# Vector operands in PSUM, another order of projections and state tiles out of the weight buffers, in a hybrid decoder step on eight cores

## The chip, the cores and the metric

One Trainium2 chip, all eight cores, the same program on each with its own sequences. The metric is the device time in microseconds (us) of the slowest core.

## The reference, cut to what matters

```python
hn = rmsnorm(x, norm1_g)
proj = hn @ w_in                        # [u | B | C | h], 2048 wide
ya = pool_mixer(u)                      # causal means of 2, 4, 8, 16 rows
yb = B * conv3(C * h)                   # gated short convolution
x  = x + concat(ya, yb) @ w_out
a  = relu(rmsnorm(x, norm2_g) @ w1)     # 1024 -> 4096
x  = x + (a * a) @ w2
y  = rmsnorm(x, final_g)
# also out: the last 15 rows of u and the last 2 of C*h per sequence (the state)
```

A core has 2128 columns (tokens), cut into five groups of 512, 480, 496, 480 and 160. All activations stay in SBUF.

## The kernel before: the parts that matter

The kernel records operations with the memory they read and write. A small scheduler derives the semaphore waits and orders each engine's queue by a cost model. TensorE keeps the program's order. A transfer's wait stands in the queue of the engine that issues it, in order with that engine's other work (in the profile before, POOL stood idle for 4.0 us until the store of npp had landed, and only then issued its next weight load).

```python
# SBUF: the weight buffers of the MLP reuse the memory of the mixer phase
R0 = cur[0]
WIN = tile((16, 8, 128), BF16); WOUT = tile((8, 1024), BF16)
HN = ...; UB = ...; UC = tile((4, 16), F32); SP = ...; ZB = ...; ZC = tile((4, 8), F32)   # state rows UC, ZC
W1B = [tile((8, 8, 128), BF16, at=R0 + i * 16384) for i in range(2)]          # over WIN
W2B = [tile((8, 1024), BF16, at=R0 + 32768 + i * 16384) for i in range(2)]    # [0] over WOUT, [1] over HN, UB, UC
A2 = ...                                                                     # over SP, ZB, ZC
# ... cut
def bank():                      # eight rotating PSUM banks
    b = nbank[0] % 8
# ... cut
def rstd(s, hl, rs, n, rq=None): # sum of squares -> broadcast by ones-matmul -> Ln, Exp, into SBUF (rs)
def conv(c, z, h, s, n, cv):     # c: block, cv: accumulator in SBUF
    act(cv, z(h - 2 * s, h - 2 * s + n), scale=cw(0, c))                       # ACT
    stt(cv, z(h - s, h - s + n), cw(1, c), cv, ALU.mult, ALU.add)              # DVE
    stt(cv, z(h, h + n), cw(2, c), cv, ALU.mult, ALU.add)                      # DVE
# ... cut
# IN(g): 16 projections; evacuations are held until the norm is known (hook), then released
IN(1, {4: lambda: rstd1(1), 9: lambda: norm1(2), 12: ..., 13: ...}, 4, 4)
# ... cut: after IN(4): store UC -> npp, ZC -> ncp (the state of the prompt)
def w1_step(...):
    act(r, bk(0, n), AF.Relu)                                                  # ACT, PSUM -> SBUF
    tt(a2[fc, 0:n], r, r, ALU.mult)                                            # DVE
def finish(g):                   # final norm
    for k in range(8):
        if k % 2:
            act(x, x, scale=fg(k))
            tt(x, x, RSF[0:n], ALU.mult, eng="gpsimd")                         # POOL
        else:
            stt(x, x, fg(k), RSF[0:n], ALU.mult, ALU.mult)                     # DVE
```

TensorE's order is IN(0), IN(1), OUT(0), IN(2), OUT(1), IN(3), OUT(2), IN(4), OUT(3), OUT(4), then 20 steps of W1 and 20 of W2 (four blocks of weights by five groups, W2 one step behind W1), with the final norms in the last steps.

## Time and profile before

| | before |
|---|---|
| time, median of the first 6 runs | 699.41 us (697.98 to 781.55, the last a slow run by its time) |
| spans of the cores in the profiled run | 691.7 to 698.8 us |
| PE / DVE / ACT / POOL busy on the slowest core | 659.8 / 403.6 / 234.2 / 185.6 us |

PE is TensorE's matmuls, DVE VectorE, ACT ScalarE, POOL GpSimd. PSUM is the memory that the matmuls write; the kernel uses it as eight banks of 512 columns, and evacuating a bank means reading it out so that the next projection may have it. The granted clock is the share of TensorE's full clock that the trace records. PE is nearly full, so the useful question is where it is not. The prediction cuts the span by stretches. To compare kernels I use a second cut, made from the traces: all 3,589 weight loads of PE are in each trace, in program order, so the n-th belongs to the same matmul of the same stage in both kernels, projections aside. A stage begins at the start of its first weight load; each start is the median over the eight cores, and a stage is the difference of two such starts.

### The profile page before, as it was taken

To read this page: it belongs to the slowest core of one execution; us is meant where nothing else is said; L and a number is where in the kernel's file an instruction comes from. 1 tells how busy PE (TensorE), PEld (TensorE's weight loads), DVE (VectorE), ACT (ScalarE), POOL (GpSimd) and SP (SyncE) were. 2 spreads that over 40 slices of the span, in tenths; PEclk is the share of its full clock that TensorE was granted. 3 is DMA by queue.
4 is the path that set the end of the run, shared out by engine and by line. 5 is a ranking of instruction groups with operands and counts; after the bars stand their busy time and mean duration, and the time that the engine had idled before them with its cause. 6 is when DMAs were issued, how large, how long until landed. Compare 5 with 4: busy or idle time off the path is not lost.

```text
span 698.8 us, 11070 instructions; the slowest of 8 cores (691.7 to 698.8 us)
## 1 busy us (share of the span) xinstructions
PE 659.8 (94%) x3586; PEld 333.6 (48%) x3589; DVE 403.6 (58%) x630; ACT 234.2 (34%) x503; POOL 185.6 (27%) x177
## 2 busy tenths in 40 slices
PE   6998999899899699999999999999999999999964
PEld 2343444344664244445644446464444655444444
DVE  4598789998892643444433444344434443475676
ACT  4585546254444202101221121121211122544553
POOL 0347859172754000001000001000000000454784
PEclk9999999999999889999999999999999999999996
DMA  8997030100199900006060002332000000030215
GB/s 248 322 290 140 1 113 12 60 0 2 30 141 153 163 1 1 0 2 121 1 121 1 0 1 44 78 60 62 1 1 1 1 1 2 0 117 1 113 63 206
DMA packets 14679, 46.76 MB, mean 67 GB/s; under 512 B 3360, under 2 KB 5920, under 8 KB 13344
## 3 DMA queue, kind: packets, MB, share of 16 engines
q0 software_dynamic: 4032, 18.88, 16.2%
q1 hardware_dynamic: 10592, 27.19, 11.9%
q8 instruction: 30, 0.49, 0.3%
q14 instruction: 25, 0.20, 0.1%
HBM read 55.69 MB, written 9.24 MB: 93 GB/s over the span
## 4 chain that ended last, share of the span: by engine, by line
PE 75%; DMA 12%; DVE 5%; issue 4%; ACT 2%; POOL 1%; DVEq 0%; ACTq 0%; SPq 0%; POOLq 0%
PE psall L385 75%; DMA big<-w 4%; DMA npp<-big 3%; DVE big L400 3%; DMA big<-w_in 2%; DVE big L409 2%; ACT big L395 2%; DMA big<-x 1%; POOL big L400 1%; DMA big<-w0c 1%; ACT big L433 0%; ACT L433 0%; DVE big L427 0%; DVEq L229 0%; DVEq L248 0%
## 5 line engine op out<-in xcount | busy, mean ns | idle before, releaser
L385 PE MATMUL psall<-big 128*128 128x480 bf16 (+3 forms) x3586 | 659.8, 346 | 33.2 <-DVE big L400 10.6
L385 PEld LDWEIGHTS psall<-big 128*128 128x128 bf16 x3589 | 333.6, 99 | 359.0 <-issue 58.0
L400 POOL TENSOR_TENSOR big<-big 128x496 f32<-128x496 f32 (+8 forms) x141 | 165.6, 1189 | 243.7 <-ACT big L395 219.0
L400 DVE TENSOR_TENSOR big<-psall,big 128x480 f32<-128x480 f32 (+7 forms) x256 | 146.6, 589 | 120.0 <-PE psall L385 110.9
L400 DVE TENSOR_TENSOR big<-big 128x496 bf16<-128x496 f32 (+5 forms) x193 | 126.6, 662 | 152.3 <-ACT big L395 142.3
L395 ACT ACTIVATE big<-psall 128x480 f32<-128x480 f32 (+5 forms) x215 | 107.9, 512 | 316.6 <-PE psall L385 296.8
L395 ACT ACTIVATE big<-big 128x480 f32<-128x480 f32 (+9 forms) x203 | 110.1, 566 | 115.6 <-DVE big L400 75.8
L409 DVE SCALAR_TENSOR_TENSOR big<-big 128x496 bf16<-128x496 f32 (+9 forms) x151 | 121.9, 847 | 9.6 <-POOL big L400 4.3
L439 POOL DMA_DIRECT2D big<-w x24 | 13.0, 545 | 239.5 <-PE psall L385 235.2
L433 ACT COPY big<-big 128x16 f32<-128x16 f32 (+1 forms) x72 | 12.4, 191 | 14.8 <-DVE big L409 6.1
L427 DVE TENSOR_TENSOR_SCAN big<-big 128x480 f32<-128x480 f32 (+3 forms) x10 | 13.7, 1375 | 3.3 <-ACT big L395 3.3
L433 ACT CAST big<-big 128x1024 bf16<-128x1024 f32 x12 | 12.4, 1042 | 6.4 <-DMA big<-w_in 6.4
L434 POOL CAST big<-big 128x1024 bf16<-128x1024 f32 x4 | 4.9, 1214 | 26.9 <-DMA big<-w_in 26.9
L418 DVE TENSOR_SCALAR big<-big 128x512 bf16<-128x512 f32 (+2 forms) x16 | 6.7, 439 | 6.4 <-DMA big<-w0c 4.4
L433 ACT ACT_TABLE_LOAD x1 | 1.3, 1283 | 6.3 <-DMA big<-w0c 6.3
L439 POOL DMA_DIRECT2D big<-w_out x4 | 2.3, 582 | 0.0
L484 DVE MEMSET big<- 128x512 bf16 x1 | 0.5, 485 | 1.2 <-PEq L264 1.2
L264 POOL MEMSET const-float32-0.0<- 128x1 f32 x1 | 0.1, 98 | 0.5 <-issue 0.5
L483 DVE MEMSET big<- 128x128 bf16 x1 | 0.2, 165 | 0.0
L777 DVE MEMSET big<- 128x128 f32 x1 | 0.2, 165 | 0.0
L264 POOL MEMSET const-bfloat16-1.0<- 128x1 bf16 x1 | 0.1, 101 | 0.0
L264 POOL MEMSET const-uint8-127<- 128x1 uint8 x1 | 0.1, 101 | 0.0
(2 smaller groups left out, 0.2 us busy)
## 6 DMA issues: line engine op xcount, KB each, us to landing
big<-w POOLq DMA_DIRECT2D x16, 512.0 KB, 11.2
big<-w POOLq DMA_DIRECT2D x8, 1024.0 KB, 17.7
big<-w_in SPq DMA_DIRECT2D x15, 512.0 KB, 9.7
y<-big SPq DMA_DIRECT2D x8, 496.0 KB, 2.8
y<-big SPq DMA_DIRECT2D x8, 480.0 KB, 2.6
big<-x SPq DMA_DIRECT2D x4, 512.0 KB, 9.1
big<-w_out POOLq DMA_DIRECT2D x4, 512.0 KB, 15.2
big<-x SPq DMA_DIRECT2D x1, 1984.0 KB, 11.2
```

The source lines that it names most:

```text
L264: nc = bass.Bass("TRN2", target_bir_lowering=False)
L385: return P.add("tensor", lambda e: e.matmul(out=out.ap, lhsT=w.ap, rhs=x.ap, start=start, stop=stop), reads=[w, x], writes=[out], cost=pas ...
L395: return P.add("scalar", lambda e: e.activation(out=out.ap, in_=in_.ap, func=func, scale=sc, **kw), reads=reads, writes=[out], cost=0.155 ...
L400: return P.add(eng, lambda e: e.tensor_tensor(out=out.ap, in0=a.ap, in1=b.ap, op=op), reads=[a, b], writes=[out], cost=cost)
L409: return P.add("vector", lambda e: e.scalar_tensor_tensor(out=out.ap, in0=a.ap, scalar=sv, in1=b.ap, op0=op0, op1=op1), reads=reads, write ...
L418: return P.add(eng, lambda e: e.tensor_scalar(out=out.ap, in0=a.ap, scalar1=sv, scalar2=None, op0=ALU.mult), reads=reads, writes=[out], co ...
L427: return P.add("vector", lambda e: e.tensor_tensor_scan(out=out.ap, data0=a.ap, data1=b.ap, initial=iv, op0=ALU.add, op1=ALU.subtract), re ...
L433: return P.add(eng, lambda e: e.copy(out=out.ap, in_=a.ap), reads=[a], writes=[out], cost=0.17 + n / 1180)
L434: return P.add(eng, lambda e: e.tensor_copy(out=out.ap, in_=a.ap), reads=[a], writes=[out], cost=0.15 + n / 960)
L439: op = P.add(q, lambda e: e.dma_start(out=out.ap, in_=src), writes=[out], cost=0.6 if q == "gpsimd" else 0.6, dma=True, nbytes=nbytes, aft ...
L483: P.add("vector", lambda e: e.memset(ONES[:].ap, 1.0 / D), writes=[ONES[:]], cost=0.2)
L484: P.add("vector", lambda e: e.memset(A2[0][0].ap, 0.0), writes=[A2[0][0]], cost=0.3)
```

## The change

Its intent: let DVE read and write PSUM where it read two operands from SBUF, so that its instructions no longer stretch beside POOL's (in the profile before, over all cores, 94 products of 480 columns with both operands in SBUF took 1.04 us on average with POOL busy for over 60% of their time, and 146 took 0.70 with it idle); load the second half of the network's weights without waiting for small stores; release PSUM early in group 1; shorten the tail. The core of the diff:

```diff
-E_ORDER = (3, 8, 12, 2, 9, 13, 4, 1, 10, 14, 5, 0, 11, 15, 6, 7)
+E_ORDER = (8, 12, 9, 13, 3, 2, 4, 10, 14, 5, 1, 11, 15, 6, 0, 7)
     ONES = tile((128,), BF16)
+    UC = tile((4, 16), F32)
+    ZC = tile((4, 8), F32)
     R0 = cur[0]
...
+    def bank():
+        nbank[0] += 1
+        return fixed(nbank[0] % 5)
+    NB = [fixed(5), fixed(6)]
+    CVB = fixed(7)
...
-            out = SP[c - 2, NMAX - nt:NMAX]
-            scan(out, ub(16, L), ub(16 - w, L - w), ini)
+            scan(NB[1](0, nt), raw or ub(16, L), ub(16 - w, L - w), 0.0 if g == 0 else SC[c - 2])
...
-    def conv(c, z, h, s, n, cv):
-        act(cv, z(h - 2 * s, h - 2 * s + n), scale=cw(0, c))
+    def conv(c, z, h, s, n, cv, acc):                  # acc: in bank CVB
+        act(acc, z(h - 2 * s, h - 2 * s + n), scale=cw(0, c))
...
+        raw = (2, 3) if g == 1 else ()                 # evacuated before the norm is known
...
-            stt(H2[g][k, 0:n], X[g][k, nm:nm + n], g2(k), R2N[0:n], ALU.mult, ALU.mult)
+            stt(H2[g][k, 0:n], X[g][k, nm:nm + n], g2(k), NB[0](0, n), ALU.mult, ALU.mult)
...
-            tt(a2[fc, 0:n], r, r, ALU.mult)
+            tt(a2[fc, 0:n], bk(0, n), r, ALU.mult)
...
+            if b < 2:                                  # W2 of blocks 0, 1 in order on the queue
+                if pw2[0] is not None:
+                    op.deps.setdefault(pw2[0], False)
+                pw2[0] = op
...
-            if k % 2:
-                act(x, x, scale=fg(k))
-                tt(x, x, RSF[0:n], ALU.mult, eng="gpsimd")
-            else:
-                stt(x, x, fg(k), RSF[0:n], ALU.mult, ALU.mult)
+            stt(x, x, fg(k), NB[g % 2](0, n), ALU.mult, ALU.mult)
```

Cut: two engines that read one PSUM bank are now ordered, the scheduler's model has DVE without a PSUM operand and POOL take turns (its simplification) and a slower first stretch of DMA (in the profile before 266 GB/s from 2 to 13 us, 319 from 13 to 40), and the hooks of IN(0) and IN(1) move by one.

More of the change, by code (lines that the diff above doesn't have):

```diff
@@ L99 @@
 class Op:
-    __slots__ = ("eng", "fn", "deps", "cost", "dma", "idx", "n", "succ", "alap", "sig", "count", "nbytes", "end", "raw")
+    __slots__ = ("eng", "fn", "deps", "cost", "dma", "idx", "n", "succ", "alap", "sig", "count", "nbytes", "end", "port")
 class Prog:
@@ L118, in add @@
         op.sig = False
+        op.port = not dma and (eng == "gpsimd" or eng == "vector" and not any(
+            isinstance(c, tuple) for v in reads for c in v.cells))
         deps = {}
@@ L124, in add @@
                     deps[o] = True
+                if isinstance(c, tuple):
+                    for o in self.r.get(c, ()):
+                        if o.eng != eng:
+                            deps[o] = True
         for v in writes:
@@ L170, in schedule @@
         dma_free = 0.0
+        port = [0.0]
         for o in ops:
@@ L194, in schedule @@
             _, _, o = heapq.heappop(avail[e])
+            if o.port:
+                t = max(t, port[0])
+                port[0] = t + o.cost
             free[e] = t + o.cost
             if o.dma:
-                dma_free = max(dma_free, t + o.cost + 1.6) + o.nbytes / 330e3
+                dma_free = max(dma_free, t + o.cost + 1.6) + o.nbytes / (260e3 if dma_free < 13 else 335e3)
                 o.end = dma_free + 0.7
@@ L311, in build_nc @@
     UB = tile((2, 16 + NMAX), F32)
-    UC = tile((4, 16), F32)
-    SP = tile((2, NMAX), F32)
+    SC = tile((2, 1), F32)
     ZB = tile((2, 8 + NMAX), F32)
-    ZC = tile((4, 8), F32)
     CGB = tile((2, NMAX), F32)
@@ L325, in build_nc @@
     R1N = tile((2, NMAX), F32)
-    R2N = tile((NMAX,), F32)
     assert cur[0] <= SBUF_BYTES, cur[0]
@@ L357, in build_nc @@
     HLF = tile((2, NMAX), BF16, at=o + 8 * NMAX)
-    RSFB = tile((2, NMAX), F32, at=o + 12 * NMAX)
-    o += 20 * NMAX
+    o += 12 * NMAX
     SQL = tile((2, NOUT[NG - 1]), F32, at=o)
@@ L371, in build_nc, with fixed @@
     nbank = [0]
-    def bank():
-        b = nbank[0] % 8
-        nbank[0] += 1
+    def fixed(b):
         def view(lo, hi):
@@ L398, in tt @@
     def tt(out, a, b, op=ALU.add, eng="vector"):
-        cost = 0.15 + out.n / 950 if eng == "vector" else 0.15 + out.n * 2.25e-3
+        cost = 0.15 + out.n / 950 if eng == "vector" else 0.15 + out.n * 1.8e-3
         return P.add(eng, lambda e: e.tensor_tensor(out=out.ap, in0=a.ap, in1=b.ap, op=op),
@@ L409, in stt @@
         return P.add("vector", lambda e: e.scalar_tensor_tensor(out=out.ap, in0=a.ap, scalar=sv, in1=b.ap, op0=op0, op1=op1),
-                     reads=reads, writes=[out], cost=0.2 + out.n / 950)
+                     reads=reads, writes=[out], cost=0.15 + out.n / 950)
     def ts(out, a, s, eng="vector"):
@@ L503, in sumsq, with rstd, pool_sum @@
             tt(s[0:n], s[0:n], b, eng=eng)
-    def rstd(s, hl, rs, n, rq=None):
+    def rstd(s, hl, n, rs=None, rq=None, b=NB[0]):
         act(hl[0, 0:n], s[0:n])
         tt(hl[1, 0:n], s[0:n], hl[0, 0:n], ALU.subtract)
-        b = bank()
         mm(b(0, n), ONES[:], hl[0, 0:n], True, False)
         mm(b(0, n), ONES[:], hl[1, 0:n], False, True)
-        act(rs, b(0, n), AF.Ln, bias=EPS)
+        act(b(0, n), b(0, n), AF.Ln, bias=EPS)
         if rq is not None:
-            act(rq, rs, AF.Exp, scale=-1.0)
-        act(rs, rs, AF.Exp, scale=-0.5)
-    def pool_sum(g, c, ub, h, n, nt, mix):
+            act(rq, b(0, n), AF.Exp, scale=-1.0)
+        act(rs or b(0, n), b(0, n), AF.Exp, scale=-0.5)
+    def pool_sum(g, c, ub, h, n, nt, mix, raw):
         w = POOL_WIN[c]
@@ L527, in pool_sum @@
         else:
-            out = SP[c - 2, NMAX - nt:NMAX]
-            ini = 0.0 if g == 0 else SP[c - 2, NMAX - 1:NMAX]
-            scan(out, ub(16, L), ub(16 - w, L - w), ini)
-            sw = SP[c - 2, NMAX - n:NMAX]
+            scan(NB[1](0, nt), raw or ub(16, L), ub(16 - w, L - w), 0.0 if g == 0 else SC[c - 2])
+            copy(SC[c - 2], NB[1](nt - 1, nt), "scalar", 1)
+            sw = NB[1](nt - n, nt)
         stt(mix, ub(h, L), -float(w), sw, ALU.mult, ALU.add)
@@ L547, in pool_sample @@
         stt(mix, UBS[c, 240:304], -float(w), src(240, 304), ALU.mult, ALU.add)
-    def conv(c, z, h, s, n, cv):
-        act(cv, z(h - 2 * s, h - 2 * s + n), scale=cw(0, c))
-        stt(cv, z(h - s, h - s + n), cw(1, c), cv, ALU.mult, ALU.add)
-        stt(cv, z(h, h + n), cw(2, c), cv, ALU.mult, ALU.add)
+    def conv(c, z, h, s, n, cv, acc):
+        act(acc, z(h - 2 * s, h - 2 * s + n), scale=cw(0, c))
+        stt(acc, z(h - s, h - s + n), cw(1, c), acc, ALU.mult, ALU.add)
+        stt(cv, z(h, h + n), cw(2, c), acc, ALU.mult, ALU.add)
     def IN(g, hook, hold=-1, first=0):
@@ L581, in IN, with taps @@
                     mm(b(lo, n), WIN[i, k], hn[k, lo:n], k == 0, k == 7)
+            def taps(c, b, zb):
+                if g == 1:
+                    tt(zb(8, 8 + npr), zb(8, 8 + npr), rq, ALU.mult, eng="gpsimd")
+                cv = CV[c % 2, 0:npr]
+                conv(c, zb, 8, 1, npr, cv, CVB(0, npr))
+                copy(ZC[c, 6:8], zb(6 + npr, 8 + npr), "scalar", 2)
+                if ns:
+                    tt(ZBS[c, 32:96], b(npr, n), CGB[c % 2, npr:n], ALU.mult)
+                    conv(c, lambda a, z: ZBS[c, a:z], 32, 16, ns, CV[c % 2, npr:n], CVB(npr, n))
+                if defer:
+                    cv = CV[c % 2, 0:n - nm]
+                    tt(cv, cv, sub(R1N, nm, n), ALU.mult, eng="gpsimd")
             def evac(kind=kind, c=c, b=b):
@@ L592, in evac @@
                         act(ub(16, 16 + nt), b(0, nt))
-                    pool_sum(g, c, ub, 16 + nm, npr, nt, mix[c, 0:npr])
+                    pool_sum(g, c, ub, 16 + nm, npr, nt, mix[c, 0:npr], None if defer else b(0, nt))
                     copy(UC[c], ub(nt, 16 + nt), "scalar", 16)
@@ L609, in evac @@
                     tt(zb(8 - zm, 8 + npr), b(nm - zm, nm + npr), CGB[c % 2, nm - zm:nm + npr], ALU.mult)
-                    if g == 1:
-                        tt(zb(8, 8 + npr), zb(8, 8 + npr), rq, ALU.mult, eng="gpsimd")
-                    cv = CV[c % 2, 0:npr]
-                    conv(c, zb, 8, 1, npr, cv)
-                    copy(ZC[c, 6:8], zb(6 + npr, 8 + npr), "scalar", 2)
-                    if ns:
-                        tt(ZBS[c, 32:96], b(npr, n), CGB[c % 2, npr:n], ALU.mult)
-                        conv(c, lambda a, z: ZBS[c, a:z], 32, 16, ns, CV[c % 2, npr:n])
-                    if defer:
-                        cv = CV[c % 2, 0:n - nm]
-                        tt(cv, cv, sub(R1N, nm, n), ALU.mult, eng="gpsimd")
+                    return lambda: taps(c, b, zb)
                 else:
                     tt(mix[4 + c, 0:n - nm], b(nm, n), CV[c % 2, 0:n - nm], ALU.mult)
-            held.append(evac)
+            if kind in raw:
+                more = evac()
+                if more:
+                    held.append(more)
+            else:
+                held.append(evac)
             if i in hook:
@@ L628, in IN @@
                 while held:
-                    held.pop(0)()
+                    more = held.pop(0)()
+                    if more:
+                        more()
         if last:
@@ L655, in rstd1 @@
         n = NIN[g]
-        rstd(S1, HL, R1N[g % 2, 0:n], n, RQ[g % 2, 0:n] if g < 2 else None)
+        if g < 2:
+            rstd(S1, HL, n, R1N[g, 0:n], RQ[g, 0:n])
+        else:
+            rstd(S1, HL, n)
     def hn_of(g):
@@ L665, in hn_of @@
             else:
-                stt(HNG[g][k, 0:n], X[g][k], g1(k), R1N[g % 2, 0:n], ALU.mult, ALU.mult)
+                stt(HNG[g][k, 0:n], X[g][k], g1(k), NB[0](0, n), ALU.mult, ALU.mult)
     def h2_of(g):
         nm, n = GROUPS[g][0], NOUT[g]
-        rstd(Sub(S2, g % 2), HL, R2N[0:n], n)
+        rstd(Sub(S2, g % 2), HL, n)
         for k in range(8):
-            stt(H2[g][k, 0:n], X[g][k, nm:nm + n], g2(k), R2N[0:n], ALU.mult, ALU.mult)
+            stt(H2[g][k, 0:n], X[g][k, nm:nm + n], g2(k), NB[0](0, n), ALU.mult, ALU.mult)
     def fold_pool(c0):
@@ L687, in build_nc @@
     norm1(0)
-    IN(0, {3: lambda: rstd1(0)}, 3, 1)
+    IN(0, {2: lambda: rstd1(0)}, 2, 1)
     hn_of(1)
@@ L691, in build_nc @@
     load_x(2)
-    IN(1, {4: lambda: rstd1(1), 9: lambda: norm1(2), 12: lambda: fold_pool(0), 13: lambda: fold_pool(2)}, 4, 4)
+    IN(1, {5: lambda: rstd1(1), 9: lambda: norm1(2), 13: lambda: fold_pool(0), 14: lambda: fold_pool(2)}, 5, 4)
     OUT(0, {1: lambda: (rstd1(2), hn_of(2))})
@@ L710, in load_w1 @@
                 "p (c k e) -> p c k e", c=2, k=8), 128 * 8192)
+    pw2 = [None]
     def load_w2(b):
         for h in range(2):
-            load("gpsimd", W2B[b % 2][4 * h:4 * h + 4], blk(w2_d, b * 8192 + h * 4096, 4096).rearrange(
+            op = load("gpsimd", W2B[b % 2][4 * h:4 * h + 4], blk(w2_d, b * 8192 + h * 4096, 4096).rearrange(
                 "p (c e) -> p c e", c=4), 128 * 16384)
+            if b < 2:
+                if pw2[0] is not None:
+                    op.deps.setdefault(pw2[0], False)
+                pw2[0] = op
     steps = [(b, g) for b in range(NBLK) for g in range(NG)]
@@ L751, in last_rstd @@
     def last_rstd(n):
-        RSF = Sub(RSFB, (NG - 1) % 2)
-        b = bank()
+        b = NB[(NG - 1) % 2]
         for i, sv in enumerate((SFB[(NG - 1) % 2, 0:n], SQL[0], SQL[1])):
             mm(b(0, n), ONE32[:], sv, i == 0, i == 2, 4)
-        act(RSF[0:n], b(0, n), AF.Ln, bias=EPS)
-        act(RSF[0:n], RSF[0:n], AF.Exp, scale=-0.5)
+        act(b(0, n), b(0, n), AF.Ln, bias=EPS)
+        act(b(0, n), b(0, n), AF.Exp, scale=-0.5)
     def finish(g):
         nm, n = GROUPS[g][0], NOUT[g]
-        RSF = Sub(RSFB, g % 2)
         if g == NG - 1:
@@ L764, in finish @@
         else:
-            rstd(Sub(SFB, g % 2), HLF, RSF[0:n], n)
+            rstd(Sub(SFB, g % 2), HLF, n, b=NB[g % 2])
         for k in range(8):
             x = X[g][k, nm:nm + n]
-            if k % 2:
-                act(x, x, scale=fg(k))
-                tt(x, x, RSF[0:n], ALU.mult, eng="gpsimd")
-            else:
-                stt(x, x, fg(k), RSF[0:n], ALU.mult, ALU.mult)
+            stt(x, x, fg(k), NB[g % 2](0, n), ALU.mult, ALU.mult)
         for h in range(4):
```

## The prediction

> **What bounds the kernel now.** I read the page first (parts 1 and 2), then the busy time of each engine by stretches, then the waits of the middle, then the timeline of single instructions. The page says that TensorE is the bound on average.
>
> ```profile
> PE 659.8 (94%) x3586; PEld 333.6 (48%) x3589; DVE 403.6 (58%) x630; ACT 234.2 (34%) x503; POOL 185.6 (27%) x177
> ...
> PE   6998999899899699999999999999999999999964
> ...
> PEclk9999999999999889999999999999999999999996
> ```
>
> The 94% is an average: only a stretch where PE idles, or runs at a lower clock, has anything to give. So I cut the span where the PE row or the clock row dips. The columns are stretch, length, busy us and instruction count of each engine, granted clock, DMA share, GB/s.
>
> ```profile
> 53.00:61.00 8.00, 5.12 (x16) 1.90 (x16) 5.49 (x9) 5.42 (x11) 4.53 (x4) 0.79 1.02 183
> 61.00:123.00 62.00, 60.57 (x289) 27.93 (x289) 54.56 (x67) 32.41 (x86) 49.43 (x40) 1.00 0.18 54
> 123.00:155.00 32.00, 28.65 (x137) 13.08 (x136) 30.59 (x48) 13.30 (x35) 13.64 (x14) 1.00 0.08 25
> 155.00:205.00 50.00, 47.39 (x313) 26.78 (x312) 44.02 (x73) 21.49 (x65) 26.34 (x31) 1.00 0.34 49
> 205.00:235.00 30.00, 30.00 (x189) 16.46 (x187) 10.28 (x21) 10.03 (x23) 9.60 (x14) 1.00 1.05 149
> 235.00:252.00 17.00, 10.59 (x31) 3.86 (x31) 14.23 (x28) 4.87 (x10) 0.00 (x0) 0.70 0.53 96
> 252.00:671.00 419.00, 419.00 (x2298) 213.35 (x2297) 185.91 (x297) 104.42 (x191) 50.45 (x47) 1.00 0.14 31
> 671.00:699.00 28.00, 13.00 (x132) 11.24 (x129) 22.58 (x35) 9.63 (x27) 16.02 (x14) 0.75 0.42 167
> ```
>
> From 252 to 671 us, the MLP, PE is busy throughout at full clock: 419 us in which the change can win nothing. The loss sits elsewhere. A 480-column matmul takes 296.5 us / 1420 = 0.209 us of PE (the groups kept apart by shape). So 53:61 did 16 x 0.209 = 3.3 us of work in 8 us: 4.7 lost. 235:252 did 31 x 0.209 = 6.5 us in 17: 10.5 lost, partly idle and partly the 0.70 clock. Idle time in 61:205 is 1.4 + 3.3 + 2.6 = 7.3 us, with DVE busy 129 us of the 144. The tail, 671:699, does 10 us of small matmuls in 28 us and is a chain through DVE.
>
> Why does 235:252 stall? The waits between 100 and 250 us and the DMA landings (last column of the second view) tell:
>
> ```profile
> DVE big L400 <- DMA ncp<-big: 9.1, 1, 9.1
> POOL big L439 <- DMA npp<-big: 4.0, 1, 4.0
> PE psall L385 <- DMA big<-w: 3.4, 1, 3.4
> ...
> PE psall L385 <- ACT big L395: 3.0, 1, 3.0
> ```
>
> ```profile
> npp<-big SPq DMA_DIRECT2D x1, 30.0 KB, 20.2
> ncp<-big SPq DMA_DIRECT2D x1, 4.0 KB, 39.0
> ```
>
> Two tiny state stores read UC and ZC, which overlap the memory of the second W2 buffer and of the MLP's first activation buffer A2. They crawl behind the 8.4 MB of weights (8 loads of 0.52 MB, 4 of 1.05), 20 and 39 us. Until they land, the POOL queue can't issue its next weight load (4.0 us) and DVE can't write the squared ReLU (9.1 us). In POOL's order a half of W2's second block stands ahead of W2's first block, so the block that is needed first is issued last (217.3 us) and lands at 245.4.
>
> Why is DVE slow around 28 to 155 us and in the tail? The timeline shows the same 160-column square, once while POOL has a run of work, once with POOL idle (the instructions of POOL's run, then DVE's):
>
> ```profile
> 670.96 8.24 POOL L400 TENSOR_TENSOR big<-big 128x480 f32<-128x480 f32 x6 [0.20 <-ACT big L395]
> ...
> 672.63 1.36 DVE L400 TENSOR_TENSOR big<-big 128x160 bf16<-128x160 f32 x1
> ...
> 683.22 0.32 DVE L400 TENSOR_TENSOR big<-big 128x160 bf16<-128x160 f32 x1 [1.26 <-ACT big L395]
> ```
>
> 1.36 against 0.32 us. By shape, between 100 and 200 us, ops with two SBUF inputs are stretched and those with one PSUM input are not:
>
> ```profile
> L409 DVE SCALAR_TENSOR_TENSOR big<-big 128x432 f32<-128x432 f32 x8 | 9.7, 1213 | 0.8 <-ACT big L395 0.7
> L400 DVE TENSOR_TENSOR big<-psall,big 128x480 f32<-128x480 f32 x15 | 9.2, 644 | 0.0
> ```
>
> [...] granted clock 0.50 in 246:250 after the stall of 242:245, 0.61 in 57:61 after that of 54:57, so a stall costs again afterwards. [...] (uncontended 480 columns in the MLP: 659 ns from SBUF, 658 with PSUM), so moving an operand to PSUM costs no rate.
>
> **The change part by part.**
> (a) UC and ZC move out of the weight buffers, and W2's halves of blocks 0 and 1 are issued in order. This removes the 9.1 and 4.0 us waits. Is W2's first block then in time? Written as bf16, 8 W1 loads of 0.52 MB and two W2 loads of 1.05 MB make 6.3 MB. Before 205 us about 50 us x 49 GB/s = 2.4 MB landed; the other 3.9 MB at 149 GB/s take 26 us: 231 us, against PE's need at 235. So it is hidden, with about 4 us to spare. Of the 10.5 us lost I expect 9 back.
> (b) DVE operands in PSUM: both reciprocal norms, the scan's output, the convolution's accumulator, the squared ReLU. About 40 second-norm products, 24 first-norm ones and some 40 convolution steps stop contending. L409 has 151 instructions at a mean of 847 ns, where uncontended 480 columns take 0.71: roughly 0.2 us x 100 = 20 us of DVE time (an estimate from those rows), nearly all between 28 and 205 us. It is worth only what PE idles there, 7.3 us in 61:205. I count 4.5.
> (c) New order of the projections, and in group 1 gates and products are evacuated raw, before the norm is known. That attacks the stall of 53:61, where PE had filled its banks while the evacuations were held. Of 4.7 us I count 3.5.
> (d) The final norm: all eight products on DVE, none on POOL or ACT. Per 480-column group DVE gets 4 x 0.67 = 2.7 us more, about 6.5 for groups 2, 3 and 4 together; off it come the contention of the 8 squares, (831 - 320) ns x 8 = 4.1 us, of 5 sums, (675 - 330) x 5 = 1.7, of the 4 last products, (664 - 310) x 4 = 1.4, and of 8 long products, 0.45 x 8 = 3.6: 10.8 us. Net 4.3 us less DVE work in a chain that DVE carries, and POOL's sums of squares come sooner. I count 5.5.
> (e) Price: five rotating PSUM banks in place of eight. Group 0's evacuation began only at 27.7 us, while PE ran on from 19.5; a projection takes 8 x 0.213 = 1.7 us (512 columns), so with five banks PE would stop around 25 us until the first evacuation. The hook comes one projection earlier, but I charge 2 us, and 1 us for waits on the single norm and convolution banks. In the MLP five banks leave 4 x 1.65 = 6.6 us to empty one, against some 0.57 (ACT) + 0.66 (DVE): no price.
> Sum: 9 + 4.5 + 3.5 + 5.5 - 3 = 19.5 us; 699.4 - 19.5 = 680.
>
> **The rivals.**
> R1, the banks become the wait: evacuation in groups 0 to 3 is held up and PE stalls on five banks, 2 to 4 us a time[...]. For it: DVE was busy 24.97 of 25 us in 28:53, when eight banks just sufficed. Against it: DVE gets faster and group 1 evacuates raw. It would eat 10 us: about 690.
> R2, the weights still arrive last: 1.05 DMA share in 205:235 says that the queue is full, and the margin is only 4 us on an average rate. If everything ahead gets faster but the transfers don't, PE waits for W2 again, 3 to 6 us: about 685.
> R3, DVE becomes the tail's bound: 8 products a group go on it, so the tail keeps its 28 us: 685.
> R4, all goes well: the stalls vanish wholly (4.7 + 7.3 + 10.5) and the tail loses 7: 670.
>
> **Range and chances.** One rival alone leaves 684 to 690, two lead to about 692, and R4 gives 670. I take 671 to 691 as eight in ten. The 2% line is 685.4; the middle is 5 us below it and a single strong rival crosses it: faster 0.68, within 2% 0.29, slower 0.03, for the MLP's 419 us do not move and the stalls would have to double.
>
> **What would show it.** (a) is right if the page after has no wait on npp or ncp, W2's first block lands before PE asks, and the clock row has no dip near slices 13 and 14. (b) if the scalar_tensor_tensor with a PSUM operand takes 0.65 to 0.72 us with POOL busy beside it. (c) if PE has no gap over 1 us near 53 us. (d) if from the last 480-column matmul to the end is 21 to 24 us instead of 28. (e) if PE shows a gap near 25 us waiting for DVE or ACT. The prediction is wrong if the MLP stretch isn't 419 us, or if PE waits on five banks add up to more than 5 us.

## The result, and the profile after

The changed kernel takes 675.95 us (median of 8 runs, 675.34 to 677.21) against 699.39 us (median of 16 runs, three of them slow by their times: 714.50, 723.08 and 781.55). The ratio is 0.9669, 95% interval 0.9658 to 0.9679. Here and below a ratio is the mean time of one kernel's fast runs over that of the kernel before in the same rounds, so not quite the ratio of the medians quoted. Executions in which one die ran at a lower clock are left out of the means.

The page of the changed kernel, its first two parts:

```profile
PE 649.0 (96%) x3586; PEld 331.2 (49%) x3589; DVE 372.4 (55%) x650; ACT 226.0 (34%) x493; POOL 147.5 (22%) x157
...
PE   6998999999999999999999999999999999999993
...
PEclk9899999999999999999999999999999999999997
```

Slices 13 and 14 of the 40 (counted from 0), where PE and its clock dipped, are full. The 8 in slice 1 of the new clock row is no mark of the change: on this core the clock was 0.76 between 20 and 25 us, on core 4 of the same run 1.00, and core 2 of the kernel before had 0.54 between 17 and 20 us. POOL lost 38 us of busy time and DVE 31. The stretches of before, on the changed kernel (stretch, length, busy us and count of PE, PEld, DVE, ACT, POOL, clock, DMA share, GB/s; the last two are cut where the changed kernel's last steps begin):

```profile
53.00:61.00 8.00, 7.09 (x35) 3.22 (x34) 4.51 (x8) 5.91 (x12) 3.07 (x3) 1.00 0.98 180
61.00:123.00 62.00, 58.83 (x282) 27.29 (x282) 49.09 (x81) 35.17 (x97) 42.51 (x40) 1.00 0.19 55
123.00:155.00 32.00, 32.00 (x160) 15.45 (x158) 26.30 (x45) 16.81 (x47) 15.37 (x19) 1.00 0.06 22
155.00:205.00 50.00, 49.44 (x370) 30.42 (x368) 34.12 (x73) 23.28 (x64) 28.98 (x35) 1.00 0.57 76
205.00:235.00 30.00, 30.00 (x148) 14.32 (x147) 20.11 (x36) 9.72 (x19) 1.11 (x3) 1.00 0.97 158
235.00:252.00 17.00, 17.00 (x83) 7.95 (x82) 6.23 (x10) 3.50 (x6) 0.00 (x0) 1.00 0.00 1
...
645.00:674.00 29.00, 16.47 (x163) 12.42 (x161) 21.05 (x50) 10.35 (x28) 6.01 (x5) 0.83 0.41 161
```

In 235:252 there are now 83 matmuls where there were 31, and the clock is 1.00. 123:155 is full. But 61:123 idles 3.2 us where it idled 1.4: something was only moved. The stages by weight loads, in us, show it for every run:

| run | to OUT(0) | OUT(0) to W1 step 0 | W1 step 0 | W1 step 1 and W2 step 0 | MLP until W1 step 19 | steps 19, to the last norm | last norm to end |
|---|---|---|---|---|---|---|---|
| before | 77.6 | 128.7 | 13.7 | 36.5 | 409.6 | 20.9 | 7.8 |
| after | 77.6 | 121.7 | 13.7 | 26.5 | 409.6 | 13.0 | 10.7 |
| e1_move | 77.9 | 129.4 | 13.7 | 40.3 | 409.6 | 21.2 | 7.4 |
| e2_order | 78.4 | 129.2 | 13.7 | 36.9 | 409.6 | 20.9 | 7.3 |
| e3_both | 77.7 | 129.4 | 13.7 | 28.8 | 409.6 | 21.3 | 7.1 |
| e4_banks5 | 87.6 | 126.5 | 18.5 | 32.3 | 409.6 | 21.9 | 7.3 |
| e11_banks5n | 84.1 | 126.6 | 14.8 | 32.8 | 409.6 | 21.6 | 7.3 |
| e5_sbuf | 81.8 | 126.9 | 13.7 | 26.5 | 409.6 | 13.0 | 10.2 |
| e6_finish | 77.3 | 121.7 | 13.7 | 26.5 | 409.6 | 17.4 | 8.0 |
| e7_eorder | 80.5 | 121.0 | 13.7 | 26.5 | 409.6 | 13.0 | 10.5 |
| e8_norm2 | 76.4 | 121.7 | 13.7 | 26.5 | 409.6 | 13.0 | 10.3 |
| e9_tail | 76.9 | 121.7 | 13.7 | 26.5 | 409.6 | 15.7 | 9.0 |
| e12_relu | 77.5 | 121.7 | 13.7 | 26.5 | 409.6 | 13.6 | 10.2 |
| e13_combo2 | 76.3 | 121.7 | 13.7 | 26.5 | 409.6 | 15.8 | 8.3 |

From before to after: nothing up to OUT(0), 7.0 us up to the MLP, 10.0 us in the first MLP steps, nothing in 409.6 us of MLP, 7.9 us in the last steps, of which 2.9 go back after the last norm. The sum is 22.0 us of span.

Where PE still pauses, in its own timeline of the changed kernel (start, length, what, then in brackets the idle time just before and what ended it):

```profile
56.32 0.36 PE L397 MATMUL psall<-big 128*128 128x480 bf16 x1 [0.51 <-ACT big L407]
57.08 8.46 PE L397 MATMUL psall<-big 128*128 128x480 bf16 x41 [0.40 <-DVE big L412]
67.68 5.88 PE L397 MATMUL psall<-big 128*128 128x480 bf16 x27 [2.14 <-DVE big L412]
74.50 104.22 PE L397 MATMUL psall<-big 128*128 128x480 bf16 x558 [0.93 <-DVE big L412]
179.28 60.93 PE L397 MATMUL psall<-big 128*128 128x160 bf16 x371 [0.56 <-DVE psall L439]
```

The 2.3 us pause at 54 us is down to 0.5 and 0.4, but pauses of 2.1 and 0.9 us stand at 65.5 and 73.6. From 74.5 us PE runs for 104 us without a pause. And the small stores, in the DMA issues (KB, us to landing), are no faster than before. Nobody waits for them any more:

```profile
npp<-big SPq DMA_DIRECT2D x1, 30.0 KB, 41.4
ncp<-big SPq DMA_DIRECT2D x1, 4.0 KB, 21.7
```

### The profile page after: what moved, and what is told of

Its sections match the earlier page's. It is cut to its first block, busy times and chain, and to the rows that moved or that the text cites. A ratio compares the mean times of both kernels' runs of the same rounds, so it can differ in the third digit from the quotient of the medians.

```text
span 673.6 us, 11364 instructions; the slowest of 8 cores (670.7 to 673.6 us)
## 1 busy us (share of the span) xinstructions
PE 649.0 (96%) x3586; PEld 331.2 (49%) x3589; DVE 372.4 (55%) x650; ACT 226.0 (34%) x493; POOL 147.5 (22%) x157
## 3 DMA queue, kind: packets, MB, share of 16 engines
q0 software_dynamic: 4032, 18.88, 17.4%
## 4 chain that ended last, share of the span: by engine, by line
PE 90%; DVE 3%; issue 2%; POOL 2%; ACT 1%; DMA 1%; DVEq 0%; ACTq 0%; POOLq 0%
PE psall L397 90%; POOL big L412 2%; DVE big L412 1%; DVE big L421 1%; ACT big L407 1%; DMA big<-w0c 1%; DVE big L430 0%; ACT L445 0%; ACT big L445 0%; DVEq L239 0%; ACT psall L407 0%; DVE psall L439 0%; DVEq L258 0%; ACTq L258 0%; POOLq L258 0%
## 5 line engine op out<-in xcount | busy, mean ns | idle before, releaser
L397 PE MATMUL psall<-big 128*128 128x480 bf16 (+3 forms) x3586 | 649.0, 344 | 15.4 <-DVE big L412 6.4
L397 PEld LDWEIGHTS psall<-big 128*128 128x128 bf16 x3589 | 331.2, 98 | 332.9 <-issue 25.4
L412 DVE TENSOR_TENSOR big<-psall,big 128x496 f32<-128x496 f32 (+7 forms) x416 | 244.5, 594 | 274.3 <-PE psall L397 135.9
L412 POOL TENSOR_TENSOR big<-big 128x480 f32<-128x480 f32 (+9 forms) x121 | 127.9, 1069 | 249.7 <-ACT big L407 224.6
L407 ACT ACTIVATE big<-big 128x480 f32<-128x480 f32 (+5 forms) x142 | 77.4, 555 | 87.6 <-DVE big L412 73.3
L421 DVE SCALAR_TENSOR_TENSOR big<-big,psall 128x480 bf16<-128x480 f32 (+7 forms) x138 | 80.1, 620 | 4.6 <-ACT psall L407 2.2
L412 DVE TENSOR_TENSOR big<-big 128x512 f32<-128x512 f32 (+6 forms) x33 | 21.8, 661 | 5.8 <-ACT big L407 4.9
L407 ACT ACTIVATE psall<-psall 128x480 f32<-128x480 f32 (+3 forms) x28 | 14.1, 504 | 7.4 <-PE psall L397 6.6
L407 ACT ACTIVATE psall<-big 128x480 f32<-128x480 f32 (+4 forms) x24 | 13.3, 556 | 9.6 <-DVE big L412 5.3
L421 DVE SCALAR_TENSOR_TENSOR psall<-big,psall 128x480 f32<-128x480 f32 (+4 forms) x24 | 13.9, 580 | 4.4 <-ACT psall L407 4.3
L445 ACT COPY big<-big 128x2 f32<-128x2 f32 (+1 forms) x72 | 12.2, 194 | 10.8 <-DVE big L412 4.1
```

Source lines behind the costliest of these rows:

```text
L397: return P.add("tensor", lambda e: e.matmul(out=out.ap, lhsT=w.ap, rhs=x.ap, start=start, stop=stop), reads=[w, x], writes=[out], cost=pas ...
L407: return P.add("scalar", lambda e: e.activation(out=out.ap, in_=in_.ap, func=func, scale=sc, **kw), reads=reads, writes=[out], cost=0.155 ...
L412: return P.add(eng, lambda e: e.tensor_tensor(out=out.ap, in0=a.ap, in1=b.ap, op=op), reads=[a, b], writes=[out], cost=cost)
L421: return P.add("vector", lambda e: e.scalar_tensor_tensor(out=out.ap, in0=a.ap, scalar=sv, in1=b.ap, op0=op0, op1=op1), reads=reads, write ...
L445: return P.add(eng, lambda e: e.copy(out=out.ap, in_=a.ap), reads=[a], writes=[out], cost=0.17 + n / 1180)
```

## The experiments

Theory after the result: (a) the 10 us are the stores and the order of W2's loads; (b) the 7 us are DVE's freedom from contention; (c) and (e) cancel in group 0 and 1; (d) the tail's 5 us come from the final norm on DVE. The rival for each is that the new schedule, which reorders every queue, gave it. Runs e1 to e4 shared a chip and rounds, so did e5 to e8, and e9 and e11 to e13. So e5 to e13 are compared with the changed kernel through their ratios to the kernel before, not in the same rounds.

### Stores and order of the weight loads, each alone

```diff
 e1 (on before)            e2 (on before)
+    UC, ZC above R0      +    op.deps.setdefault(pw2[0], False)   # W2 halves in order
```

> The kernel before with only UC and ZC moved out of the weight buffers. My theory: the stall of 235 to 252 us has two causes, the stores that hold memory and the order of the W2 loads. Moving alone removes the 9.1 us wait of DVE on the ncp store and the 4.0 us wait of POOL on the npp store, but the second block of W2 still goes first, so W2's first block still lands last and PE still waits on it: 2 to 5 us faster than before, about 696. Rival (the stores were the whole cause): the full 10 us, about 689. Rival (the order was the whole cause): no change, 699.

> The kernel before with only the issue order of the W2 halves of blocks 0 and 1 fixed. My theory: W2's first block lands some 10 us earlier, but DVE still waits for the ncp store before it can write A2, and PE stops once its banks are full: 2 to 6 us faster, about 695. Rival (order is the whole cause): 10 us, about 689. Rival (stores are the whole cause): no change, 699.

> The kernel before with both. The ledger of the two profiles puts 10.0 us of the change's 23.4 us between the second W1 step and the third, so my theory: 10 us faster, about 689, with no wait on npp, ncp or w between 200 and 260 us. Rival (part of that gain came from the new schedule or from PSUM operands): clearly less than 10, about 694.

Measured: e1 703.14 us, ratio 1.001 (0.9993 to 1.0027). e2 701.71, ratio 0.9979 (0.9955 to 1.0003). e3 692.66, ratio 0.9865 (0.9844 to 0.9885); before took 702.81 on this chip. Alone, neither part does anything clear; together they give 1.35%, 9.5 us. The waits between 200 and 262 us (who waited for what: us in total, times, longest) show each cause standing in for the other. First e1:

```profile
PE psall L385 <- DMA big<-w: 11.7, 2, 7.6
```

Then e2:

```profile
DVE big L400 <- DMA ncp<-big: 18.8, 1, 18.8
...
PE psall L385 <- ACT big L395: 9.0, 2, 6.1
```

And e3:

```profile
PE psall L385 <- DMA big<-w: 4.0, 1, 4.0
```

In e1 the stores hold nothing, so both halves of W2's second block go out even earlier, at 192 us, ahead of the first block that PE needs next, and PE waits 11.7 us for that. In e2 W2's first block is in order, but DVE can't write A2 until the store of ncp has landed, 18.8 us; ACT and then PE back up. My expectation for e1 and e2, 2 to 6 us each, was wrong: I had added up what are two locks on one door. e3 met its 10 us but not its second half: PE still waits 4.0 us for W2. In the changed kernel it doesn't. The timelines of POOL show when the first load of W2 leaves; e3 first:

```profile
211.64 1.15 POOL L439 DMA_DIRECT2D big<-w  x2
```

Changed kernel:

```profile
201.82 0.57 POOL L451 DMA_DIRECT2D big<-w  x1
```

Measured from the same core's start of the MLP (207.4 and 200.3 us) that is 4.2 against 1.5 us; the first W1 load, too, leaves 25.5 us ahead of it instead of 22.8, on all eight cores. So some 2 us of the stage's gain come from the loads being issued earlier in POOL's queue. That last step is read from the two traces; no run isolates it.

### Contention of DVE with POOL

```diff
 e5 (on after)
-            rstd(S1, HL, n)
+            rstd(S1, HL, n, RSN[0:n])            # RSN: one SBUF tile; also in h2_of
-                stt(HNG[g][k, 0:n], X[g][k], g1(k), NB[0](0, n), ALU.mult, ALU.mult)
+                stt(HNG[g][k, 0:n], X[g][k], g1(k), RSN[0:n], ALU.mult, ALU.mult)
-                conv(c, zb, 8, 1, npr, cv, CVB(0, npr))
+                conv(c, zb, 8, 1, npr, cv, cv)   # accumulator in SBUF
```

> The changed kernel (676 us) with the reciprocal norms of both norms (groups 2 to 4 of the first, all of the second) and the convolution's accumulator back in SBUF, all else as changed. If freedom from contention with POOL gave the 7 us that PE gained between 118 and 206 us: 4 to 7 us slower than the changed kernel, about 681, PE idle between 118 and 200 us back to 4 to 6 us, and the scalar_tensor_tensor of 480 columns back at 0.8 us or more. If the new schedule, projection order and relief of POOL gave it: within 1 us of 676.

Measured: 687.3 us, ratio 0.982 (0.9796 to 0.9843), against 0.9669 for the changed kernel: some 9 to 11 us slower (by stages and by ratio), more than I expected. Of the 7.0 us between OUT(0) and the MLP, 5.2 are gone (121.7 to 126.9), and another 4.2 us are lost before OUT(0) (77.6 to 81.8), where I had expected nothing. The groups by shape between 90 and 205 us (partitions x elements, count, busy us and mean ns); first the changed kernel, one PSUM operand:

```profile
L421 DVE SCALAR_TENSOR_TENSOR big<-big,psall 128x480 bf16<-128x480 f32 x18 | 11.6, 700 | 0.8 <-ACT big L445 0.8
```

Then e5, both in SBUF:

```profile
L422 DVE SCALAR_TENSOR_TENSOR big<-big 128x480 bf16<-128x480 f32 x17 | 14.9, 909 | 0.0
```

700 against 909 ns for the same product. This edit changes both the contention and the queue order that the scheduler derives from it, so how the 9 to 11 us divide between the two is not shown. That the instruction itself gets longer is: POOL was no busier beside it (61.0 us of these 115 against 63.6 in the changed kernel). In group 1, too, on all eight cores, the convolution's 64 steps on float32 output took 1181 ns on average in e5 and 707 in the changed kernel: 0.47 us times 8 steps a core is 3.8 us of DVE beside the 4.2 lost there. And in the changed kernel's profile (all cores) 240 tensor_tensor instructions of 480 columns with one PSUM input took 655 ns on average with POOL busy for over 60% of their time, and 488 took 656 with it idle.

The prediction compared two SBUF inputs with one PSUM input (1213 against 644 ns) and left out a single SBUF input, which can be stretched as well. The changed kernel's tensor_scalar, with one SBUF tensor as input, took 0.45 us while POOL only issued loads, and 1.44 beside POOL's multiplications (over all cores, 14 of 480 columns took 0.46 us on average with POOL idle, 15 took 1.14 with it busy for over 60% of their time):

```profile
43.67 0.45 DVE L430 TENSOR_SCALAR big<-big 128x480 bf16<-128x480 f32 x1
...
47.84 1.52 POOL L412 TENSOR_TENSOR big<-big 128x496 f32<-128x496 f32 x1 [0.25 <-DVE big L421]
48.18 1.44 DVE L430 TENSOR_SCALAR big<-big 128x480 bf16<-128x480 f32 x1
```

### Five banks and the order of projections

```diff
 e4 (on before)                e11 (on before)
-        b = nbank[0] % 8     -        b = nbank[0] % 8
+        b = nbank[0] % 5     +        b = nbank[0] % 5
                               # and rstd's matmul into a bank of its own, number 5
 e7 (on after): old E_ORDER, raw = (), hooks of IN(0), IN(1) as before
```

> The kernel before with five rotating PSUM banks instead of eight, everything else unchanged. The prediction charged 2 to 3 us for this; the changed kernel shows no such price. If five banks are costly by themselves and the new order of the projections pays for it: 3 to 12 us slower, about 705, with PE gaps near 25 and 45 to 57 us. If five banks are enough in any case: 699 to 701.

e4's output is wrong (relative error 0.13): the norm of a group takes a rotating bank, with five of them the one that a held projection still occupies. Its time, 707.29 us, ratio 1.0069 (1.0046 to 1.0092), is only a hint. e11 mends it.

> The kernel before with five rotating banks and a sixth kept for the norms, which makes the earlier five-bank run (wrong in its output: a norm took the bank of a projection still held) correct. If five banks are costly without the rest of the change: 4 to 10 us slower than 699, the loss in the first two projections (before 88 us). If that loss came from the norm in the rotation: within 2 us of 699.

Measured: correct, 700.7 us, ratio 1.0032 (1.0015 to 1.0049). Within 2 us in total, but the stages say otherwise: 6.4 us are lost up to OUT(0) (77.6 to 84.1), 2.8 of them by the start of IN(1), and 4.4 come back by the end, most of it where PE waited for weights before (W1 step 1 and W2 step 0, 36.5 to 32.8). PE's timeline of e11:

```profile
26.86 27.02 PE L385 MATMUL psall<-big 128*128 128x512 bf16 x112 [3.06 <-DVE big L400]
...
62.61 15.24 PE L385 MATMUL psall<-big 128*128 128x480 bf16 x66 [3.14 <-DVE big L400]
```

> The changed kernel with the old order of projections and without raw evacuation in group 1, hooks as before; five banks stay. The ledger shows no gain up to 118 us, so if the order buys nothing: within 1 us of 676. If the order is what makes five banks enough (it pays for a price that is hidden in the ledger): 3 to 10 us slower, with PE gaps near 25 or 45 to 57 us. If the order costs something at 64 to 75 us: faster by 1 to 2 us.

Measured: 678.02 us (three fast runs; a fourth was slow, 714.09), ratio 0.9695 (0.9676 to 0.9714), some 2 us slower than the changed kernel (0.9669), though the two intervals touch; 2.9 us lost up to OUT(0), 0.7 gained after it. The loss is clear of the cores' spread: OUT(0) starts at 79.0 to 81.8 us on e7's cores, at 75.9 to 78.6 on the changed kernel's. And the gap near 25 us that the prediction charged, absent from the changed kernel, is back on all eight cores (1.3 to 2.4 us):

```profile
27.47 23.80 PE L397 MATMUL psall<-big 128*128 128x512 bf16 x112 [1.53 <-DVE big L412]
```

So the order, the raw evacuation and the hooks together do buy something, between two of my expectations.

### What binds group 1 now

```diff
 e8 (on after)
-            sumsq(X[g][k], SQ, S1, k, NIN[g], "vector" if g < 2 else "gpsimd")
+            sumsq(X[g][k], SQ, S1, k, NIN[g], "vector" if g < 3 else "gpsimd")
```

> The changed kernel with group 2's seven sums of squares on DVE instead of POOL. In the changed kernel POOL works without a break from 57.8 to 80.6 us and the chain there runs through POOL, while PE idles 3.1 us at 65.5 and 73.6 us. If POOL's load is what ate the gain expected in group 1: 2 to 3 us faster, about 673.5. If something else (x of group 1, DVE) is the bound there: within 0.7 us of 676, or slower.

The changed kernel's POOL has hardly a pause over 22.8 us there (timeline of POOL):

```profile
57.79 22.81 POOL L412 TENSOR_TENSOR big<-big 128x496 f32<-128x496 f32 x18 [8.43 <-ACT big L407]
```

Measured: 674.05 us (three fast runs; a fourth was slow, 799.96), ratio 0.9638 (0.9618 to 0.9657). PE's pauses shrink but don't go:

```profile
67.42 5.88 PE L397 MATMUL psall<-big 128*128 128x480 bf16 x28 [1.73 <-DVE big L412]
73.72 46.48 PE L397 MATMUL psall<-big 128*128 128x480 bf16 x221 [0.42 <-DVE big L412]
```

OUT(0) starts 1.2 us earlier, and from the start of IN(1) to OUT(0) e8's cores take 32.0 to 32.9 us, the changed kernel's 32.9 to 34.2. POOL's load is part of what binds there, not all; of the chain of e8 between 50 and 80 us, more runs through DVE than through POOL. One piece of it is the pooling scan, 2.0 us at 60.6: in groups 0 and 1 the change leaves it two SBUF inputs. In group 1 of the changed kernel it takes 1.81 us on average (all cores), in the later groups, with a PSUM input, 1.22 for 480 columns. That this binds PE is not shown; no run changes it.

### The tail

```diff
 e6 (on after): finish and its norm in SBUF as before
 e12 (on after)
-            tt(a2[fc, 0:n], bk(0, n), r, ALU.mult)
+            tt(a2[fc, 0:n], r, r, ALU.mult)
 e9 (on after): in finish, for groups 2 and 3
+            if k % 2 and g in (2, 3):
+                act(x, x, scale=fg(k))
+                tt(x, x, RSFB[g % 2, 0:n], ALU.mult, eng="gpsimd")
```

> The changed kernel with the final norm as before: reciprocal norm in SBUF, odd blocks scaled on ACT and multiplied on POOL. If moving the final norm to DVE and PSUM gave the tail's 5 us: about 680 to 682. If the squared ReLU's PSUM operand alone gave it (its 160-column instructions no longer wait for POOL): within 1.5 us of 676.

> The changed kernel with the squared ReLU computed from SBUF twice (r times r), as before, all else as changed, the final norm on DVE included. The old final norm cost only 0.7 us, so the tail's 5 us must come from elsewhere. If the PSUM operand of the squared ReLU is what helps: the last W1 step gets 3 to 6 us longer only if POOL still works beside it; POOL now only sums squares of group 3 there, so 0.5 to 3 us slower than 676. If either measure alone is enough (POOL's work gone, or the PSUM operand): within 1 us of 676, and no change in the MLP's 419 us.

> The changed kernel with the odd blocks of the final norm of groups 2 and 3 back on ACT and POOL (POOL reads a copy of the reciprocal norm in SBUF), the even blocks and all of the last group on DVE with the PSUM operand. In the changed kernel's tail the DVE drains 16 products after the last matmul while POOL is idle. If DVE is what ends the kernel: 1.5 to 3 us faster than 676, about 673.8. If the mix brings the contention back, or the last group's own chain ends the kernel: within 1 us of 676 (the kernel with the old final norm took 0.7 us more).

Measured: e6 676.73 us (three fast runs; a fourth was slow, 726.37), ratio 0.968 (0.9654 to 0.9705). e12 675.16 us, ratio 0.9664 (0.9648 to 0.9679). e9 676.71, ratio 0.9685 (0.9668 to 0.9702). None differs clearly from the changed kernel. By stages, from W1 step 19 to the end: before 28.7, after 23.7, e6 (squared ReLU from PSUM, old final norm) 25.4, e12 (new final norm, old ReLU) 23.8. So either measure brings most of the 5 us and the new norm all of it. The groups of DVE after 648 us show why. First e6, whose POOL still multiplies: the square reads PSUM and escapes (316 ns), the sum of squares (first line) has two SBUF inputs and doesn't (622):

```profile
L413 DVE TENSOR_TENSOR big<-big 128x160 f32<-128x160 f32 x5 | 3.1, 622 | 0.1
...
L413 DVE TENSOR_TENSOR big<-psall,big 128x160 bf16<-128x160 f32 x8 | 2.3, 316 | 1.2 <-ACT big L408 1.2
```

Then e12, whose POOL has little left to do:

```profile
L412 DVE TENSOR_TENSOR big<-big 128x160 bf16<-128x160 f32 x8 | 2.7, 384 | 0.3 <-ACT big L407 0.3
...
L412 DVE TENSOR_TENSOR big<-big 128x160 f32<-128x160 f32 x5 | 1.6, 322 | 0.2
```

In the profile before, the sum cost 675 ns and the square 831. e9 tried to hand half of the products back to POOL, which idles at the end. It failed: its sums cost 677 ns again, steps 19 grow by 2.7 us (13.0 to 15.7) and only 1.7 come off after the last norm.

### An attempt to beat both

e13 is e9's tail, e8's sums on DVE, and half of group 1's products by the reciprocal mean on DVE.

> An attempt to beat both: the changed kernel with group 2's sums of squares on DVE, half of group 1's products by the reciprocal mean on DVE, and the tail of the run above. If the gains add: 676 - 2 (sums) - 2 (tail) - 0 to 1 (products) = about 671.5. If DVE becomes the bound in group 1 instead of POOL: 673 to 675.

Measured: 675.11 us, ratio 0.9665 (0.965 to 0.968): no gain. OUT(0) starts at 76.3 us, as in e8, and the tail of e9 takes it back. e8 alone is the fastest kernel, 0.3% below the changed one; the two were timed in different rounds and their intervals nearly touch, so call it 0 to 3 us.

## Why the prediction was right

The time predicted was 680 us, the range 671 to 691, the chance of over 2% faster 0.68; measured 675.95. The total was near partly because errors cancelled.

- (a) predicted 9 us, measured 10.0 in the stage. Right in mechanism: no wait on either store is left, W2 arrives in time, the clock doesn't dip. e3 shows that this part by itself gives 9.5 us of time. What the prediction did not say, and e1 and e2 show, is that its two halves are worth nothing apart.
- (b) predicted 4.5 us, the mis-sized term. Between OUT(0) and the MLP 7.0 us were gained, and e5 takes 5.2 of them back (4.5 as the median of each core's own stage); no run says what gave the rest. I had counted only what PE idled there; e5 shows that the operands also carry 4.2 us before OUT(0), so 9.4 in all, the new queue order included. The predicted duration, 0.65 to 0.72 us beside a busy POOL, was right: 0.700 and, for 496 columns, 0.721.
- (c) predicted 3.5 us, and no gap over 1 us near 53. There is none there, but pauses of 2.1 and 0.9 us stand at 65.5 and 73.6, and the stage up to OUT(0) gained nothing. Group 1 by itself did shrink: from the start of IN(1) to OUT(0), per core, from a median of 34.9 us to 33.3, so up to 1.6 us of the 3.5 (the cores range from 32.8 to 35.3 and from 32.9 to 34.2). Against the same kernel with the old order, e7, the order and the raw evacuation are worth 2.9 us; what ate it is the next point.
- (e) predicted a price of 2 us near 25 and 1 us elsewhere. The gap near 25 did not come: the first evacuation starts at 25.3 us in the changed kernel instead of 27.7 (medians over the cores 23.7 and 25.8). e7 shows it where only order, raw evacuation and hooks are the old ones, so it is they that avoid it; e11 shows it where all the rest of the change is missing, 3.06 us at the very place, and 6.4 us in all up to OUT(0). So five banks cost twice what I charged there, and (c) and the convolution's PSUM accumulator pay for it: 6.4 - 2.9 - 4.2 = -0.7, measured 0.0. The terms come from different kernels, so this sum is a plausibility, not a proof. In the changed kernel PE's waits for ACT and DVE between 55 and 75 us add up to 4.0 us, less than the 5 that would have refuted the prediction.
- (d) predicted 5.5 us, measured 5.0 (28.7 to 23.7). Right. DVE drains 16 products after the last matmuls, and the time after the last norm grew from 7.8 to 10.7 us.
- The MLP: 409.6 us from W1 step 2 to W1 step 19 in all fourteen profiles. Right.
- Rivals: R1 is real but was paid for; R2 shows in e3 (4.0 us) and not in the changed kernel; R3 shows in the time after the last norm; R4, 670 us, did not come, for group 1 kept its pauses.

What stays open: why e11 regains 4.4 of its 6.4 us (the stages say where, not by which wait), and what besides POOL binds group 1 at 65 us (the scan on two SBUF inputs is a candidate).

## What to carry to other kernels

Two waits that guard the same moment must be removed together: measure the pair before judging either part worthless (here 9.5 us for the pair, nothing clear for either alone). On an elementwise chain that runs beside GpSimd, count the SBUF inputs of each VectorE instruction; turning the second into a PSUM operand took 0.2 us off the 480-column product between 90 and 205 us (909 to 700 ns), and more in group 1 (1181 to 707 for the convolution's steps). One SBUF input is not safe by itself: look at the durations beside POOL, as for the tensor_scalar here (0.45 us while POOL only issued loads, 1.44 beside its multiplications). Before giving PSUM banks to such operands, ask when the first evacuation starts: the banks that remain must carry TensorE to that time (with five, TensorE in e11 waited 3.06 us near 25 us for the first evacuation; in the changed kernel, whose evacuation starts at 25.3 us instead of 27.7, that gap did not come).

## Also measured

- A PSUM operand cost no time: in the MLP the 480-column square took 657 ns with a PSUM operand (the changed kernel) and 665 ns from SBUF (e12).
- In the changed kernel's profile TensorE was busy for all of the 393 us from 252 to 645 us on every core, with random data, and the granted clock there was 1.00 on each. Every fast execution listed with its cores has a mean clock of 0.97 or more on each core. The lower clock came in some executions only: in the slow one of e6, e7 and e8, the lowest core had 0.91, 0.93 and 0.82, each time on one die.
- Over five profiles (before, after, e1, e2, e3) the store of 4 KB took 21.7 to 47.0 us and that of 30 KB 20.2 to 41.4 us to land beside 8.4 MB of weights.
